# Moving the tiles of a transformer layer onto lines of 128 bytes, with one set of operands 64 bytes off

## The chip, the cores and the metric

The kernel runs on one core of one Trainium2 chip. The metric is the time of one execution on the device in microseconds (us), from three runs. One further execution was recorded by the hardware profiler; every row of a trace in this document is from such a profiled execution. A place in the on-chip memory (SBUF) is given as the byte address inside one of its 128 partitions; "32 mod 128" means that the address leaves 32 when divided by 128.

## The reference, cut to what matters

One layer of an encoder over 512 tokens of width 2048, all in fp32:

```python
mod = silu(c) @ w_ada + b_ada                    # six vectors of 2048: sh1, sc1, g1, sh2, sc2, g2
h = rms_norm(x, norm1_g) * (1.0 + sc1) + sh1
proj = h @ w_in                                  # 2048 x 7168
o_hg = hgrn2_mixer(...)                          # 8 heads of 128, gated linear recurrence
o_sb = stick_breaking_mixer(...)                 # 8 heads of 128, causal attention
x = x + g1 * (concatenate([o_hg, o_sb], -1) @ w_out)
h = rms_norm(x, norm2_g) * (1.0 + sc2) + sh2
gate, up = split(h @ w_ffn_in, 2)                # 2048 x 11264: the first feed-forward product
x = x + g2 * ((silu(gate) * up) @ w_ffn_out)     # 5632 x 2048: the second
```

## The kernel before, in words

**Products in two halves.** Each large product is made of fp32r matmuls. Both operands are split into a high part (rounded to fp32r) and a low part (the rest), and each piece of the product is three matmuls: high by high, high by low, low by high (`three`, `product`, `multiply`). The weights come in by DMA as fp32 into one of four raw tiles (`raw_tile`, L171); `split` (L212 to L222) makes the high part on ScalarE (L220) and the low part on VectorE (L221). The split weights go into a ring of three tiles `hi` and three tiles `lo` in the pool `wp`. In the first feed-forward product every fourth split goes instead into the pair `hi2`, `lo2` of the pool `tp`, which lies at the other end of SBUF (`spare_here`, L1105). The trace calls these operands ff_3hi and ff_3lo, where those of the ring are ff_3h and ff_3l. In the second product every fourth split goes into an unused part of the tile `opsB` (`spare_there`, L1165).

**Stages, in order.** (1) `st`: the hg values for all heads, 16 steps of 24 matmuls with 512 columns, while the first vector of the modulation is computed. (2) `sbp`: eight projections for the attention heads, 1,536 matmuls with 384 columns, with the attention itself between them. (3) `hgf`, `hgq`, `hgg`: projections for the recurrent heads, 1,152 matmuls with 512 columns, with the recurrence between them. (4) `wo`: the output projection, 720 matmuls with 512 columns and, for its last tile, 96 with 256. (5) `ff`, `ffA`, `ffB`, `ffC`: the first feed-forward product, for the tile pairs f = 0 and 1 as 384 plain matmuls, for f = 2 to 43 with Strassen's seven products in place of eight (the operands 1 to 7 of the table `H`), each of 24 matmuls with 256 columns: 42 x 7 x 24 = 7,056. (6) `foA`, `foB`, `foC`: the second feed-forward product in the same way, 1,848 matmuls with 512 columns, and the output.

In stages 3 to 5 a matmul's stationary operand (the one loaded into the array) is a split weight, and its moving operand (the one streamed past it) is an activation: `hhi`/`hlo`, `ohi`/`olo`, `opA` to `opD`. In stages 1, 2 and 6 it is the other way round, and the weight moves. `opA` to `opD` are the seven Strassen operands; `opsA` to `opsC` are those of the second product. Several of these share a place: `hhi`, `ohi`, `opB`, `opsC` in tag `hhi`; `hlo`, `olo`, `opC`, `opsB` in `hlo`; `opA`, `opsA` in `b1`; `opD`, `yraw` in `b22`.

**Places.** Pools are laid down from the left end of SBUF in the order in which they are opened, those with `side="right"` from the right end, and each tile is rounded up to 32 bytes. In the compiled program of this kernel the operands lie thus:

| tiles | first address | mod 128 |
|---|---|---|
| raw tiles | 11,040 | 32 |
| `hi`, `lo` (six tiles of 4,096 bytes) | 43,808 | 32 |
| `hhi`, `ohi`, `opB`, `opsC` | 68,384 | 32 |
| `hlo`, `olo`, `opC`, `opsB` | 101,152 | 32 |
| `opA`, `opsA` | 133,920 | 32 |
| `opD` | 166,688 | 32 |
| `hi2`, `lo2` | 215,008 and 219,104 | 96 |
| `ffS` (sums of weight halves) | 195,552 | 96 |
| `xo`, `x1`, `O` (right end) | 196,576 | 96 |

Inside these tiles every operand of a matmul starts a multiple of 512 bytes from the tile's start, so that its place mod 128 is that of its tile.

The order of the instructions on each engine is fixed when the program is built. On TensorE's queue the small matmuls of attention and recurrence are put between those of the projections by a planner (`Clock`, `Timed`, the times in `Y`) which knows nothing of places.

Of the kernel before, what the change touches and what calls it, by code (L numbers as in the profile page):

```python
# [10 lines left out]
F32 = mybir.dt.float32  # L11
F32R = mybir.dt.float32r
# [5 lines left out]
P = 128  # L18
D = 2048
KT = 16  # L20
T = 512
# [3 lines left out]
HT = 256  # L25
HALF = 8
CHUNKS = (3, 3, 4, 4, 4, 4)
ORDER = (2, 1, 7, 6, 4, 5, 3)
AHEAD = 300
SC2_EARLY = 8  # L30
HG_TASKS = 8
EARLY = 3
# [3 lines left out]
EPS = 1e-6  # L36
# [93 lines left out]
def trunk(ctx, tc, a):  # L130
    nc = tc.nc
    V, S, G = nc.vector, nc.scalar, nc.gpsimd
# [2 lines left out]

    const = ctx.enter_context(tc.tile_pool(name="const", bufs=1))
    wp = ctx.enter_context(tc.tile_pool(name="wp", bufs=3))
    xctx = ctx.enter_context(ExitStack())
    xop = xctx.enter_context(tc.tile_pool(name="xop", bufs=1, side="right"))
    hp = ctx.enter_context(tc.tile_pool(name="hp", bufs=1))  # L140
    dram = ctx.enter_context(tc.tile_pool(name="dram", bufs=1, space=bass.MemoryType.DRAM))
    psum = ctx.enter_context(tc.tile_pool(name="psum", bufs=4, space=bass.MemoryType.PSUM))

    def acc(name):
        return psum.tile([P, T], F32, tag="acc", name=name)
# [9 lines left out]
    ones = const.tile([P, P], F32, name="ones")  # L155
    G.memset(ones, 1.0)
    one = ones[:, 0:1]
    epsb = const.tile([P, 1], F32, name="epsb")
    G.memset(epsb, EPS)
    lead = const.tile([P, 2], F32, name="lead")  # L160
    left = [KT] * 6
    mod = const.tile([P, 96], F32, name="mod")
    gain1 = const.tile([P, KT], F32, name="gain1")
# [48 lines left out]
    def split(r, shape, name):  # L212
# [3 lines left out]
        else:  # L216
            hi = wp.tile(shape, F32R, tag="hi", name=name + "h")
            lo = wp.tile(shape, F32R, tag="lo", name=name + "l")
        with tc.high_priority(offset=AHEAD):
            S.copy(hi, r)  # L220
# [32 lines left out]
        newton(y, av, tmp)  # L253


    hhi = hp.tile([P, KT, T], F32R, tag="hhi", name="hhi")
    hlo = hp.tile([P, KT, T], F32R, tag="hlo", name="hlo")
    xo = xop.tile([P, KT, T], F32, tag="xo", name="xo")
    vctx = ctx.enter_context(ExitStack())
    vp = vctx.enter_context(tc.tile_pool(name="vp", bufs=1))  # L260
# [531 lines left out]
        gates[h] = SG  # L792


    ohi = hp.tile([P, KT, T], F32R, tag="hhi", name="ohi")
    olo = hp.tile([P, KT, T], F32R, tag="hlo", name="olo")
    last = NH - 1

    def split_o(k):
# [36 lines left out]
    fh = ctx.enter_context(tc.tile_pool(name="fh", bufs=1, reuse_waits="tile"))  # L836
    fg = ctx.enter_context(tc.tile_pool(name="fg", bufs=1, reuse_waits="tile"))
# [35 lines left out]

    early = fh.tile([P, 2, HALF, 2, HT], F32R, tag="b1", name="opA")
    H = {1: early[:, 0], 2: early[:, 1], 3: fg.tile([P, HALF, 2, HT], F32R, tag="b22", name="opD")}
    parts = {}

    def block(kh, th, j):  # L880
# [42 lines left out]
    for i, hs in enumerate(halves):  # L923
        out = acc(f"wo{m}h{i}")[:, 0:HT]
        n = 0
# [55 lines left out]
            with tc.high_priority(offset=AHEAD):  # L981
                hold(0)

    late = hp.tile([P, 2, HALF, 2, HT], F32R, tag="hhi", name="opB")
    later = hp.tile([P, 2, HALF, 2, HT], F32R, tag="hlo", name="opC")
    H.update({6: late[:, 0], 7: late[:, 1], 5: later[:, 0], 4: later[:, 1]})
    for j in range(HALF):
        V.tensor_sub(block(0, 0, j), block(0, 1, j), block(0, 0, j))
# [33 lines left out]
    places, blocks = [], [{} for _ in units]  # L1022
# [19 lines left out]
    yraw = []  # L1042

    def begin_second():
        places.append(fh.tile([P, 4, 4, 2, HT], F32R, tag="b1", name="opsA"))
        load_op(0, 0)
        load_y(0, 2)
        load_op(0, 1)
        load_y(0, 0)
        yraw.append(hp.tile([P, 3, 4, T], F32, tag="hhi", name="yraw0"))  # L1050
        load_y(0, 1)
        load_y(0, 3)
        load_op(0, 2)
        load_op(0, 3)
        places.append(hp.tile([P, 4, 4, 2, HT], F32R, tag="hlo", name="opsB"))
        for q in range(4, 7):
            load_op(0, q)
        yraw.append(fg.tile([P, 2, 4, T], F32, tag="b22", name="yraw"))

    rest += [partial(ada, G2, k) for k in range(KT)]  # L1060

# [37 lines left out]
    later = []  # L1099
# [9 lines left out]
    count[0] = 0  # L1109
    with tc.high_priority(offset=AHEAD):  # L1110
        hold(1)
# [118 lines left out]
    for u, (c, i) in enumerate(units):  # L1230
# [15 lines left out]
        for q, p in enumerate(ORDER):  # L1246
# [37 lines left out]
            if p == 3:  # L1284
                load_y(u + 1, 3)
            if u == 0 and q == 6:
                places.append(hp.tile([P, 4, 4, 2, HT], F32R, tag="hhi", name="opsC"))
            if q < 4 and i == (c == 0):
                load_op(c + 1, q)
            if i == 1 and 1 <= q < 4:  # L1290
# [61 lines left out]
```

## Time and profile before

| | |
|---|---|
| median of three runs | 2299.24 us (2299.24 to 2306.46) |
| the profiled execution | 2301.37 us |
| its span, first to last instruction | 2299.2 us |
| mean granted TensorE clock | 0.994 |
| busy: TensorE, weight loads, VectorE, ScalarE | 98%, 89%, 83%, 50% of the span |

Matmuls are pipelined: in the trace one with 256 columns lasts some 280 ns, but the next starts long before it ends. What a matmul costs is the distance from its start to the next one's start, and it is read from the first column of the timeline.

### The profile page before, as it was taken

The page shows a single profiled execution, that of the slowest core. Times are in us where ns is not written, and L with a number is a line of the kernel's source. Part 1 is how long each engine was busy: PE and PEld are TensorE (multiplying, and loading weights), DVE is VectorE, ACT ScalarE, POOL GpSimd, SP SyncE. Part 2 cuts the span into 40 slices and gives each one's busy share as a digit, 9 for nine tenths or more (in the row PEclk, how much of TensorE's full clock was granted, in tenths as well). Part 3 has the DMA queues.
Part 4 walks back from the last instruction along what each step waited for, and adds up shares of the span by engine and source line. Part 5 has one row for each costly group of instructions (what it writes and reads, how often), then busy time and mean ns, then how long its engine had stood idle before and what let it go on. Part 6 is the DMA issues. An engine that isn't in the chain of part 4 may idle for free.

```text
span 2299.2 us, 35729 instructions
## 1 busy us (share of the span) xinstructions
PE 2249.4 (98%) x14171; PEld 2050.2 (89%) x14171; DVE 1917.8 (83%) x2566; ACT 1160.6 (50%) x2015; POOL 10.7 (0%) x25
## 2 busy tenths in 40 slices
PE   7999899999999999999999999999999999999999
PEld 6899899888888788999999999999999977778787
DVE  8887779999888865699899988888888778888888
ACT  4316666565655522564454445454545544544453
POOL 0000000000000000000000000000000000000000
PEclk9999999999999999999999999999999999999999
DMA  9885546853322386346555645454443486665452
GB/s 368 319 317 218 174 145 227 304 183 111 128 93 74 130 303 214 105 151 225 189 204 185 220 143 175 143 174 143 150 160 129 166 314 232 238 220 213 154 200 76
DMA packets 114978, 437.69 MB, mean 190 GB/s; under 512 B 9822, under 2 KB 58236, under 8 KB 76796
## 3 DMA queue, kind: packets, MB, share of 16 engines
q1 hardware_dynamic: 114812, 435.42, 53.0%
q8 instruction: 111, 1.82, 0.3%
q14 instruction: 55, 0.45, 0.1%
HBM read 386.61 MB, written 48.77 MB: 189 GB/s over the span
## 4 chain that ended last, share of the span: by engine, by line
PE 77%; DVE 13%; DMA 3%; issue 3%; ACT 3%; SPq 0%; DVEq 0%; ACTq 0%
PE ffA L93 18%; PE foA L93 9%; PE ffC L93 9%; PE sbp L93 7%; PE wo L93 7%; PE foC L93 4%; PE ffB L93 4%; PE st L93 4%; PE hgf L93 4%; PE hgq L93 3%; PE hgg L93 3%; DMA opd<-fhi 1%; DVE ada L180 1%; DVE yraw L1190 1%; PE l L93 1%
## 5 line engine op out<-in xcount | busy, mean ns | idle before, releaser
L180 DVE SCALAR_TENSOR_TENSOR ada<-ada,cond 128x2048 f32<-128x2048 f32 x95 | 216.8, 2286 | 54.5 <-DMA ada<-in_w_ada 54.3
L93 PE MATMUL ffA<-opD,ff_3h 128*128 128x256 f32 x512 | 93.9, 284 | 1.8 <-ACT u L1018 1.7
L93 PE MATMUL ffA<-opB,ff_6h 128*128 128x256 f32 x512 | 94.1, 284 | 1.0 <-ACT ff_6h L220 1.0
L93 PE MATMUL ffB<-opA,ff_2h 128*128 128x256 f32 x512 | 93.5, 283 | 0.0
L93 PE MATMUL ffC<-opC,ff_4h 128*128 128x256 f32 x512 | 93.5, 283 | 0.0
L93 PE MATMUL ffA<-opC,ff_5h 128*128 128x256 f32 x496 | 90.7, 283 | 0.8 <-ACT b L1018 0.8
L93 PE MATMUL ffA<-opA,ff_1h 128*128 128x256 f32 x496 | 90.6, 283 | 0.0
L93 PE MATMUL ffC<-opB,ff_7h 128*128 128x256 f32 x496 | 90.6, 283 | 0.0
L221 DVE TENSOR_TENSOR wfo_0l<-wfo,wfo_0h 128x1024 fp32r<-128x1024 f32 x48 | 58.7, 1224 | 37.9 <-ACT wfo_0h L220 37.5
L93 PEld LDWEIGHTS ffA<-opD,ff_3h 128*128 128x128 f32 x512 | 79.7, 192 | 2.4 <-ACT u L1018 2.4
L93 PEld LDWEIGHTS ffA<-opB,ff_6h 128*128 128x128 f32 x512 | 80.1, 193 | 1.3 <-ACT ff_6h L220 1.2
L93 PEld LDWEIGHTS ffC<-opC,ff_4h 128*128 128x128 f32 x512 | 79.7, 192 | 0.0
L93 PEld LDWEIGHTS ffB<-opA,ff_2h 128*128 128x128 f32 x512 | 79.7, 192 | 0.0
L220 ACT CAST wfo_0h<-wfo 128x1024 fp32r<-128x1024 f32 x48 | 50.6, 1054 | 57.5 <-PE foA L93 50.4
L1092 ACT CAST fhi<-forms 128x512 fp32r<-128x512 f32 (+1 forms) x63 | 43.6, 692 | 68.5 <-DMA opd<-fhi 59.2
L93 PEld LDWEIGHTS ffA<-opC,ff_5h 128*128 128x128 f32 x496 | 77.2, 192 | 1.0 <-ACT b L1018 1.0
L93 PEld LDWEIGHTS ffC<-opB,ff_7h 128*128 128x128 f32 x496 | 77.3, 192 | 0.0
L93 PEld LDWEIGHTS ffA<-opA,ff_1h 128*128 128x128 f32 x496 | 77.2, 192 | 0.0
L93 PE MATMUL ffA<-opB,ff_6l 128*128 128x256 f32 x256 | 72.7, 284 | 0.0
L93 PE MATMUL ffC<-opC,ff_4l 128*128 128x256 f32 x256 | 72.4, 283 | 0.0
L93 PE MATMUL ffA<-opD,ff_3l 128*128 128x256 f32 x256 | 72.4, 283 | 0.0
L93 PE MATMUL ffB<-opA,ff_2l 128*128 128x256 f32 x256 | 72.4, 283 | 0.0
(1646 smaller groups left out, 7764.6 us busy)
## 6 DMA issues: line engine op xcount, KB each, us to landing
ada<-in_w_ada SPq DMA_DIRECT2D x95, 1024.0 KB, 5.2
wfo<-in_w_fo SPq DMA_DIRECT2D x16, 1024.0 KB, 5.9
yraw<-in_w_fo SPq DMA_DIRECT2D x16, 1024.0 KB, 4.8
fix<-in_w_fix SPq DMA_DIRECT2D x14, 1024.0 KB, 5.6
opd<-forms SPq DMA_DIRECT2D x44, 256.0 KB, 4.3
opd<-fhi SPq DMA_DIRECT2D x42, 256.0 KB, 4.3
opsC<-opd SPq DMA_DIRECT2D x10, 1024.0 KB, 5.1
opsA<-opd SPq DMA_DIRECT2D x9, 1024.0 KB, 7.2
```

The costliest lines, as they stand in the source:

```text
L93: self.engine.matmul(out, lhsT, rhs, **kw)
L180: V.scalar_tensor_tensor(w, w, 1.0, row, op0=ALU.mult, op1=ALU.mult, accum_out=col)
L220: S.copy(hi, r)
L221: V.tensor_sub(lo, r, hi.bitcast(F32))
L1092: S.copy(hi, R[:, q])
L1190: V.tensor_sub(*(t[:, k0:k0 + w] for t in (d, e, g)))
```

## The change

A pool `edge` of 96 bytes is opened first at the right end; the constant `epsb` moves into it. `lead` grows from 2 to 34 elements. The tiles for the operands get 32 elements (128 bytes) more than they hold, and a new function returns a view that begins a given number of elements into such a tile: 16 elements (64 bytes) for `opA` to `opD`, none for all others. No instruction is added, removed or moved.

```diff
+ROOM = 32
+OFF_H, OFF_O, OFF_F, OFF_X = 0, 0, 16, 0
...
+    edge = ctx.enter_context(tc.tile_pool(name="edge", bufs=1, side="right"))
...
+    def offset(pool, shape, dtype, tag, name, shift):
+
+        n = int(np.prod(shape[1:]))
+        t = pool.tile([P, n + ROOM], dtype, tag=tag, name=name)[:, shift:shift + n]
+        axes = "abcd"[:len(shape) - 1]
+        sizes = dict(zip(axes, shape[1:]))
+        return t.rearrange(f"p ({' '.join(axes)}) -> p {' '.join(axes)}", **sizes)
...
-    epsb = const.tile([P, 1], F32, name="epsb")
-    G.memset(epsb, EPS)
-    lead = const.tile([P, 2], F32, name="lead")
+    epsw = edge.tile([P, 24], F32, name="epsw")
+    G.memset(epsw, EPS)
+    epsb = epsw[:, 0:1]
+    lead = const.tile([P, 34], F32, name="lead")
...
-    hhi = hp.tile([P, KT, T], F32R, tag="hhi", name="hhi")
-    hlo = hp.tile([P, KT, T], F32R, tag="hlo", name="hlo")
+    hhi = offset(hp, [P, KT, T], F32R, "hhi", "hhi", OFF_H)
+    hlo = offset(hp, [P, KT, T], F32R, "hlo", "hlo", OFF_H)
...
-    ohi = hp.tile([P, KT, T], F32R, tag="hhi", name="ohi")
-    olo = hp.tile([P, KT, T], F32R, tag="hlo", name="olo")
+    ohi = offset(hp, [P, KT, T], F32R, "hhi", "ohi", OFF_O)
+    olo = offset(hp, [P, KT, T], F32R, "hlo", "olo", OFF_O)
...
-    early = fh.tile([P, 2, HALF, 2, HT], F32R, tag="b1", name="opA")
-    H = {1: early[:, 0], 2: early[:, 1], 3: fg.tile([P, HALF, 2, HT], F32R, tag="b22", name="opD")}
+    early = offset(fh, [P, 2, HALF, 2, HT], F32R, "b1", "opA", OFF_F)
+    H = {1: early[:, 0], 2: early[:, 1], 3: offset(fg, [P, HALF, 2, HT], F32R, "b22", "opD", OFF_F)}
...
-    late = hp.tile([P, 2, HALF, 2, HT], F32R, tag="hhi", name="opB")
-    later = hp.tile([P, 2, HALF, 2, HT], F32R, tag="hlo", name="opC")
+    late = offset(hp, [P, 2, HALF, 2, HT], F32R, "hhi", "opB", OFF_F)
+    later = offset(hp, [P, 2, HALF, 2, HT], F32R, "hlo", "opC", OFF_F)
...
-        places.append(fh.tile([P, 4, 4, 2, HT], F32R, tag="b1", name="opsA"))
+        places.append(offset(fh, [P, 4, 4, 2, HT], F32R, "b1", "opsA", OFF_X))
...
```

`opsB`, `opsC` and the two `yraw` tiles are changed in the same way, with an offset of 0.

## Rows read from the trace of the kernel before

**Rows 1.** Page, parts 1 and 2: busy time of each engine, and the granted clock.

```profile
PE 2249.4 (98%) x14171; PEld 2050.2 (89%) x14171; DVE 1917.8 (83%) x2566; ACT 1160.6 (50%) x2015; POOL 10.7 (0%) x25
...
PEclk9999999999999999999999999999999999999999
```

**Rows 2.** Page, part 4: the chain that ended last, shares of the span.

```profile
PE 77%; DVE 13%; DMA 3%; issue 3%; ACT 3%; SPq 0%; DVEq 0%; ACTq 0%
```

**Rows 3.** Busy time by stretch: PE, PEld, DVE, ACT, POOL; then clock, DMA share, GB/s.

```profile
0.00:100.00 100.00, 88.22 (x382) 72.66 (x383) 83.50 (x126) 44.67 (x59) 1.68 (x9) 1.00 0.95 354
...
440.00:770.00 330.00, 327.22 (x1674) 274.89 (x1672) 288.25 (x540) 200.90 (x444) 9.05 (x16) 1.00 0.36 131
770.00:950.00 180.00, 177.28 (x820) 146.16 (x818) 111.03 (x137) 54.59 (x85) 0.00 (x0) 1.00 0.62 218
950.00:1015.00 65.00, 60.57 (x489) 59.13 (x488) 63.43 (x154) 54.00 (x124) 0.00 (x0) 1.00 0.27 94
...
1400.00:1849.00 449.00, 449.00 (x3796) 449.00 (x3796) 364.66 (x412) 224.82 (x326) 0.00 (x0) 1.00 0.46 159
1849.00:2299.00 450.00, 435.61 (x1917) 352.05 (x1916) 379.23 (x433) 211.91 (x269) 0.00 (x0) 0.99 0.56 201
```

**Rows 4.** Timeline of TensorE, first feed-forward product: start us, us, then engine, line, operands, count.

```profile
1303.62 0.40 PE L93 MATMUL ffA<-opC,ff_5h 128*128 128x256 f32 x2
...
1306.50 0.39 PE L93 MATMUL ffC<-opC,ff_4hi 128*128 128x256 f32 x2
...
1309.11 0.28 PE L93 MATMUL ffC<-opC,ff_4lo 128*128 128x256 f32 x1
```

**Rows 5.** Timeline of TensorE, output projection, 512 columns.

```profile
850.18 0.39 PE L93 MATMUL wo<-olo,wo_8h 128*128 128x512 f32 x1
850.40 0.39 PE L93 MATMUL wo<-ohi,wo_8l 128*128 128x512 f32 x1
...
852.90 0.39 PE L93 MATMUL wo<-olo,wo_0h 128*128 128x512 f32 x1
```

**Rows 6.** Timeline of TensorE, attention projection, 384 columns.

```profile
149.97 0.33 PE L93 MATMUL sbp<-wsb_2h,hhi 128*128 128x384 f32 x1
...
151.53 0.33 PE L93 MATMUL sbp<-wsb_2h,hhi 128*128 128x384 f32 x1
```

**Rows 7.** Timeline of TensorE where the clock is at half: two groups, 256 columns.

```profile
1016.21 0.63 PE L93 MATMUL ffC<-opB,ff_7hi 128*128 128x256 f32 x2
1016.64 0.41 PE L93 MATMUL ffC<-opB,ff_7lo 128*128 128x256 f32 x1
...
1018.13 0.63 PE L93 MATMUL ffA<-opB,ff_6h 128*128 128x256 f32 x2
1018.56 0.41 PE L93 MATMUL ffA<-opB,ff_6l 128*128 128x256 f32 x1
```

**Rows 8.** Busy time and clock in that stretch.

```profile
1015.80:1018.70 2.90, 2.90 (x15) 2.90 (x15) 2.90 (x3) 0.42 (x1) 0.00 (x0) 0.50 0.00 0
```

**Rows 9.** Timeline of TensorE: a plain fp32 group of the recurrence, 256 columns.

```profile
511.45 1.03 PE L93 MATMUL r<-QB_w,KB_w 128*128 128x256 f32 x4
```

**Rows 10.** Groups by line: count, busy us, mean ns of one, idle before.

```profile
L93 PE MATMUL r<-QB_w,KB_w 128*128 128x256 f32 x8 | 2.0, 378 | 0.0
L93 PE MATMUL ffA<-opC,ff_5h 128*128 128x256 f32 x496 | 90.7, 283 | 0.8 <-ACT b L1018 0.8
L93 PE MATMUL ffA<-opC,ff_5hi 128*128 128x256 f32 x176 | 30.6, 277 | 0.0
```

**Rows 11.** Timeline of the weight loads, output projection (compare group 5).

```profile
850.18 0.19 PEld L93 LDWEIGHTS wo<-ohi,wo_8l 128*128 128x128 f32 x1
850.41 0.19 PEld L93 LDWEIGHTS wo<-ohi,wo_0h 128*128 128x128 f32 x1
```

**Rows 12.** Groups by line: the two splits, from tiles at 96 and at 32 mod 128.

```profile
L221 DVE TENSOR_TENSOR wfo_0l<-wfo,wfo_0h 128x1024 fp32r<-128x1024 f32 x48 | 58.7, 1224 | 37.9 <-ACT wfo_0h L220 37.5
L220 ACT CAST wfo_0h<-wfo 128x1024 fp32r<-128x1024 f32 x48 | 50.6, 1054 | 57.5 <-PE foA L93 50.4 <-PE ffC L93 2.4 <-DVE wfo_2l L221 2.0
L221 DVE TENSOR_TENSOR ff_5l<-ffS,ff_5h 128x1024 fp32r<-128x1024 f32 x31 | 37.8, 1218 | 0.0
L220 ACT CAST ff_5h<-ffS 128x1024 fp32r<-128x1024 f32 x31 | 32.5, 1050 | 36.6 <-PE ffA L93 36.6
```

**Rows 13.** Busy time by stretch inside the first feed-forward product, columns as in group 3.

```profile
1200.00:1300.00 100.00, 99.94 (x842) 99.72 (x842) 91.93 (x103) 48.49 (x71) 0.00 (x0) 1.00 0.54 195
...
1500.00:1600.00 100.00, 100.00 (x848) 100.00 (x847) 82.42 (x93) 50.73 (x74) 0.00 (x0) 1.00 0.47 161
```

More of the change, by code (lines that the diff above doesn't have):

```diff
@@ L1049, in begin_second @@
         load_y(0, 0)
-        yraw.append(hp.tile([P, 3, 4, T], F32, tag="hhi", name="yraw0"))
+        yraw.append(offset(hp, [P, 3, 4, T], F32, "hhi", "yraw0", 0))
         load_y(0, 1)
@@ L1054, in begin_second @@
         load_op(0, 3)
-        places.append(hp.tile([P, 4, 4, 2, HT], F32R, tag="hlo", name="opsB"))
+        places.append(offset(hp, [P, 4, 4, 2, HT], F32R, "hlo", "opsB", OFF_X))
         for q in range(4, 7):
             load_op(0, q)
-        yraw.append(fg.tile([P, 2, 4, T], F32, tag="b22", name="yraw"))
+        yraw.append(offset(fg, [P, 2, 4, T], F32, "b22", "yraw", 0))
     rest += [partial(ada, G2, k) for k in range(KT)]
@@ L1286, in trunk @@
             if u == 0 and q == 6:
-                places.append(hp.tile([P, 4, 4, 2, HT], F32R, tag="hhi", name="opsC"))
+                places.append(offset(hp, [P, 4, 4, 2, HT], F32R, "hhi", "opsC", OFF_X))
             if q < 4 and i == (c == 0):
```

## The prediction

> **What bounds the kernel now.** I read the shares first: TensorE is busy 98% of the span at a clock that is nearly always full [rows 1], and the chain of work that ended last runs over TensorE for 77%, over VectorE for 13% [rows 2]. The stretches say the same stage by stage: in the second half of the first feed-forward product TensorE is busy 449.00 of 449 us, in the output projection 177 of 180, in the second feed-forward product 436 of 450 [rows 3]. Two stretches differ. In the first 100 us the DMA engines are busy 95% at 354 GB/s, beside a TensorE busy 88%; from 950 to 1015 us VectorE is busy 63.43 of 65 us [rows 3]. So outside those two, what a matmul costs is what the kernel costs.
>
> What a matmul costs is read from starts. In the first feed-forward product a group of 24 with weights from the ring (place 32 mod 128, moving operand at 32 too) goes from 1303.62 to 1306.50 us: 2.88 / 24 = 120.0 ns each. The next group has its weights in `hi2`, `lo2` (96, moving operand still at 32): from 1306.50 to the start of its last at 1309.11 there are 23 distances, 2.61 / 23 = 113.5 ns [rows 4]. 256 columns at 2.4 GHz take 106.7 ns, so the excess is 13.3 ns (32 cycles) in the first group and 6.8 ns (16 cycles) in the second. With 512 columns and both operands at 32, twelve distances take 2.72 us, 226.7 ns each, against 213.3: again 13.3 [rows 5]. With 384 columns nine take 1.56 us, 173.3 against 160: again 13.3 [rows 6]. The excess is thus the same per matmul at every width, and it halves when the two operands lie 64 bytes apart mod 128. The groups show that this is no accident of one product: 283 ns for 496 matmuls, 277 for 176 of the other kind [rows 10]. Where the clock is at half, two matmuls take 0.43 us, 215 ns each, in both kinds, and 213.3 is what 256 columns need at 1.2 GHz [rows 7, 8]. In plain fp32, four records take 1.03 us, the last of them 378 ns by its group, so three distances take 0.65 us, 217 ns, for 256 columns at two cycles each [rows 9, 10]. [...]
>
> **The change part by part.** No instruction is added or removed; addresses move. `epsb` leaves the left end and `lead` grows from 32 to 160 bytes, so all that follows on the left goes up by 96: 11,040 becomes 11,136 = 87 x 128, and raw tiles and the ring lie on lines; each operand tile then takes 128 bytes more, and the later ones stay on lines. At the right end `edge` pushes everything down by 96: from 96 to 0 mod 128, `hi2` and `lo2` too. So the first feed-forward product gets weights at 0 and moving operands at 64, all other fp32r products 0 and 0.
>
> *First feed-forward product, 7,056 matmuls of 256 columns.* Every fourth of the 294 splits goes to `hi2`: 73 x 24 = 1,752 matmuls at 113.5, the other 5,304 at 120.0, sum 835.3 us, which with few waits is the stage that ends at 1849 us. The new pair (0, 64) is nowhere in the trace. Its distance is the cheap one, so at most 113.5; the 16 cycles that then remain have one candidate left, the start in the middle of a 64-byte piece (32 and 96 both are), and it goes too. The lower bound is 106.7 plus the 2 to 3 ns that the slow streams keep; I take 109.3. That is 771.2 us, 64.1 less; the bounds are 35 (113.5 for all) and 82 (106.7). VectorE eats some of it: up to f = 17 it also does a modulation row for each f and is busy 91.93 of 100 us [rows 13]. An f takes 168 matmuls, 19.84 us now, with 18.2 us of VectorE; at 109.3 it takes 18.36, and VectorE would be at 99%. It can't be that dense with its waits on ScalarE's high parts, so I give back 0.25 us for each of 16 f: 60 us are left. From f = 18 it is busy 82.42 of 100, which becomes 89% and hides.
>
> *The 384 plain matmuls before it* stand in the stretch where VectorE is busy 63.43 of 65 us [rows 3]: of up to 4 us I take 1. *The last output tile*, 96 matmuls of 256 columns: 1 us.
>
> *All others, 0 and 0.* The start is mended, the distance is not. [...] If that still costs, 6.7 ns are saved per matmul; if it cost only because the moving stream had a piece too many, all but 2.6 ns go: 10.7. Both come from the rows above and nothing is nearer; I take the middle, 8.7 ns (for 384 columns too).
> - Attention projections: 1,536 x 8.7 = 13.4 us; attention stands between them, I keep 80%: 10.7.
> - `st`: 384 x 8.7 = 3.3, but DMA is busy 95%: 1 [rows 3].
> - Recurrent projections: 1,152 x 8.7 = 10.0; VectorE is busy 288 of 330 us: 7 [rows 3].
> - Output projection: 720 x 8.7 = 6.3; VectorE has room (111 of 180): 6 [rows 3].
> - Second feed-forward product: 1,848 x 8.7 = 16.1; VectorE is busy 379 of 450: 14 [rows 3].
>
> *VectorE, ScalarE, DMA.* Their operands move too. The splits cost 1224 and 1054 ns from tiles at 32, 1218 and 1050 from a tile at 96 [rows 12]: within half a percent, so nothing. The transfers keep their sizes; nothing. `epsb` and `lead` are touched a few times: nothing, and were a few tenths of a us lost, the DMA wait at the start would hide it.
>
> Sum: 60 + 1 + 1 + 10.7 + 1 + 7 + 6 + 14 = 101 us. The profiled execution took 2301.4 us (span 2299.2), 2 above the median of the runs, so the median goes to 2299.2 - 101 = **2198 us**.
>
> [...] With weights at 96 in place of 32 and nothing else changed, a matmul is 6.5 ns shorter [rows 4]; so the weight's place reaches the moving stream. [...]
>
> **The rivals.**
> - *Only the distance counts, not the line.* All of the first feed-forward product comes to 113.5 (5,304 x 6.5 = 34 us), the 0-and-0 products stay as they are: 2264 us with a us for the plain 384. For it: distance is all that the rows vary. Against it: an excess of 16 cycles would be left in a pair that lies well.
> - *Two streams on one line collide for the whole 32 cycles.* Only the 64-byte offset gains: 61 us, 2238.
> - *64 bytes is half a line of 128.* The first feed-forward product stops at 113.5 and the rest gains: 34 + 40 = 74 us, 2225.
> - *The pair at the other end of SBUF is cheap because of its region, and no place mod 128 matters.* Then nothing changes: 2299. For it: `hi2` is the only tile at 96 that feeds a matmul here, and it lies some 170,000 bytes from the ring. Against it: exactly 16 cycles.
> - *Slower: the weight's own place sets the price.* 96 costs 16 cycles and 32 costs 32, so by a straight line 0 costs 40 (16.7 ns): ring products lose 3.3 ns, `hi2` products 9.9, the 5,640 others 3.3: 17.5 + 17.3 + 18.6 = 53 us, 2352. It decides once weights at 0 cost over 28 cycles, today's mean of the first feed-forward product; nothing shows 0.
>
> **How the numbers follow.** Forecast 0.52, distance alone 0.15, collision 0.12, half line 0.07, nothing 0.08, slower 0.06. The forecast by itself spans 2172 (10.7 for the others, nothing lost to VectorE) to 2210 (6.7 and more lost). Going up, the range takes in 2225, 2238 and 2264; leaving out 2299 and 2352 (0.14) and a little at the low end gives 2172 to 2266. Some 0.3% is what a measurement here tells from no change. Faster: 0.52 + 0.15 + 0.12 + 0.07 = 0.86; same 0.08; slower 0.06.
>
> **What would show it.** In the profile after, groups of 24 in the first feed-forward product should take 2.62 us, ring and `hi2` alike; 2.72 means distance alone or half a line, 2.88 nothing. Output projection matmuls should start 216 to 220 ns apart; 226.7 means the collision. VectorE should be busy over 97% between 1000 and 1300 us, with waits of TensorE on the low parts. The prediction is wrong if TensorE's distances shrink and its waits on VectorE take the gain back, or if they don't shrink.

## The result, and the profile after

The changed kernel took 2311.3 us (median of six runs, 2307.61 to 2312.69) beside 2303.38 us for the kernel before (six runs, 2299.24 to 2306.46; the first three of them are those shown above): ratio 1.0035, 95% interval 1.0023 to 1.0046. It is slower by a third of a per cent, where a time 4.4% under the median shown was forecast. The profiled execution took 2311.36 us, span 2309.2 us.

The page, part 1, and the shares of the chain that ended last:

```profile
PE 2253.2 (98%) x14171; PEld 2037.6 (88%) x14171; DVE 1915.4 (83%) x2566; ACT 1156.1 (50%) x2015; POOL 10.8 (0%) x25
...
PE 69%; DVE 17%; DMA 7%; issue 4%; ACT 3%; SPq 0%; DVEq 0%; ACTq 0%
```

Counts and shares are those of before, to the instruction [rows 1]; each engine also has the same instructions in the same order. But TensorE's part of the chain fell from 77 to 69%, and DMA's rose from 3 to 7% [rows 2]: something new waits on transfers. Busy time by stretch (PE, PEld, DVE, ACT, POOL, then clock, DMA share, GB/s):

```profile
770.00:950.00 180.00, 176.30 (x775) 140.94 (x774) 110.57 (x135) 55.45 (x87) 0.00 (x0) 1.00 0.60 212
...
1400.00:1849.00 449.00, 445.27 (x3806) 442.67 (x3806) 368.62 (x419) 223.31 (x329) 0.00 (x0) 1.00 0.45 154
```

In the second half of the first feed-forward product TensorE has 3,806 matmuls where it had 3,796, and is idle 3.7 us where it was never idle [rows 3]. In the output projection's window it is nearly as busy (176.3 us for 177.3) and has fewer, 775 for 820; part of that is the stage's start, 3 us later.

The matmuls themselves, from the timeline of TensorE (start us, duration us, engine, line, operands, count). First feed-forward product, a group with `opB`, then one with `opC`:

```profile
1308.87 0.40 PE L95 MATMUL ffC<-opB,ff_7h 128*128 128x256 f32 x2
...
1311.70 0.40 PE L95 MATMUL ffA<-opC,ff_5h 128*128 128x256 f32 x2
...
1314.43 0.39 PE L95 MATMUL ffC<-opC,ff_4hi 128*128 128x256 f32 x2
```

From 1308.87 to 1311.70 there are 24 distances with `opB`: 2.83 us, 117.9 ns each. From 1311.70 to 1314.43 there are 24 with `opC`: 2.73 us, 113.8 each. The ring and `hi2` no longer differ; which moving operand a group has now decides. 2.62 us for 24, as forecast, is nowhere. VectorE, forecast to be busy over 97% from 1000 to 1300 us, was busy 276.2 of the 300. Output projection, 512 columns:

```profile
854.94 0.40 PE L95 MATMUL wo<-olo,wo_0h 128*128 128x512 f32 x1
855.18 0.39 PE L95 MATMUL wo<-ohi,wo_0l 128*128 128x512 f32 x1
855.41 0.40 PE L95 MATMUL wo<-ohi,wo_0h 128*128 128x512 f32 x1
...
857.74 0.40 PE L95 MATMUL wo<-olo,wo_0h 128*128 128x512 f32 x1
```

Twelve distances take 2.80 us, 233.3 ns, against 226.7 before [rows 5] and 216 to 220 forecast: a loss.

Stage by stage, from the start of a stage's first matmul to that of its last, in us:

| stage | before | after | lines_only | off_lines | room_256 |
|---|---|---|---|---|---|
| `st`, 512 columns | 88.7 | 91.5 | 89.7 | 91.2 | 89.0 |
| `sbp`, 384 columns | 338.3 | 335.6 | 335.8 | 335.4 | 335.7 |
| recurrent projections, 512 | 327.9 | 330.2 | 328.2 | 330.2 | 327.2 |
| output projection, 512 | 173.2 | 177.1 | 173.1 | 178.7 | 173.2 |
| first feed-forward product, 256 | 893.4 | 893.4 | 902.5 | 890.5 | 892.3 |
| second feed-forward product, 512 | 445.5 | 448.9 | 445.3 | 447.7 | 445.3 |

After against before: +2.8 - 2.7 + 2.3 + 3.9 + 0 + 3.4 = 9.7 us, of the 10.0 between the two profiled executions. Each column is one execution, and a stage can differ by some 3 us from one to the next without any change in its matmuls: the output projection took 176.1 us in `before_two_fhi` (below), whose matmuls there cost 227.0 ns as before. The prices are steadier. The mean distance between starts of neighbouring matmuls of a stage, those over 245 ns left out, went from 226.7 to 231.7 ns in `st`, from 228.2 to 231.8 in the recurrent projections, from 227.0 to 233.0 in `wo` and from 227.5 to 229.7 in the second feed-forward product. So two things are to be explained: why products of 512 columns lose, and why 256 columns gain nothing although their matmuls got shorter.

### The profile page after: what moved, and what is told of

Read it like the earlier page. It is cut to its first block, busy times and chain, and to the rows that moved or that the text cites. A ratio compares the mean times of both kernels' runs of the same rounds, so it can differ in the third digit from the quotient of the medians.

```text
span 2309.2 us, 35729 instructions
## 1 busy us (share of the span) xinstructions
PE 2253.2 (98%) x14171; PEld 2037.6 (88%) x14171; DVE 1915.4 (83%) x2566; ACT 1156.1 (50%) x2015; POOL 10.8 (0%) x25
## 4 chain that ended last, share of the span: by engine, by line
PE 69%; DVE 17%; DMA 7%; issue 4%; ACT 3%; SPq 0%; DVEq 0%; ACTq 0%
PE ffA L95 11%; PE sbp L95 9%; PE foA L95 9%; PE wo L95 7%; PE ffC L95 6%; PE foC L95 4%; PE st L95 4%; PE hgf L95 4%; PE hgq L95 3%; PE hgg L95 3%; DMA opd<-fhi 3%; PE ffB L95 3%; DVE yraw L1202 1%; PE l L95 1%; DVE ff_5l L233 1%
## 5 line engine op out<-in xcount | busy, mean ns | idle before, releaser
L1104 ACT CAST fhi<-forms 128x512 fp32r<-128x512 f32 (+1 forms) x63 | 43.7, 693 | 123.9 <-DMA opd<-fhi 88.4
L1105 DVE TENSOR_TENSOR forms<-forms,fhi 128x512 fp32r<-128x512 f32 (+1 forms) x63 | 48.9, 776 | 37.7 <-ACT fhi L1104 37.5
```

The source lines that it names most:

```text
L1104: S.copy(hi, R[:, q])
L1105: V.tensor_sub(R[:, q].bitcast(F32R), R[:, q], hi.bitcast(F32))
```

## The experiments

In what follows the distance is the place of the moving operand less that of the stationary one, mod 256 bytes. "Lateness" is worked out from the 7,056 starts of the Strassen part of the first feed-forward product: all distances between starts over 124 ns, each less the mean of the rest, summed; the mean of the rest is the "mean matmul". Lateness is more than waiting. Of the changed kernel's 26.9 us, 19.3 stand at starts before which TensorE sat idle for over 0.12 us. Another 2.1 stand at the start next after such a wait, which comes some 222 ns after it, and 3.1 in two stretches at a granted clock of 0.50, from 1021.7 and from 1113.8 us, both soon after waits of 2.6 to 2.8 us; the kernel before has one such stretch there, from 1015.5 us.

**Does the line of 128 bytes do anything?** In `lines_only` every operand lies on a line and none is 64 bytes off:

```diff
-ROOM = 32
-OFF_H, OFF_O, OFF_F, OFF_X = 0, 0, 16, 0
+ROOM = 64
+OFF_H, OFF_O, OFF_F, OFF_X = 0, 0, 0, 0
```

> The changed kernel with 256 spare bytes per operand tile in place of 128 and no offset anywhere: all tiles on lines, every pair of operands at distance 0 mod 256. If the line counts, as the prediction had it: 512 columns at 216 to 220 ns, 384 at 163 to 167, some 30 to 50 us faster than before. If only the distance counts: 512 columns at 226.7 and 384 at 173 to 174 as before, the first feed-forward product at 120.0 in all products; the quarter that was cheap loses 6.6 ns x 1,752 = 11.6 us, so the kernel comes out some 10 us slower than before (about 2311).

2310.27 us, ratio 1.0043 (1.0026 to 1.0059). Timelines of TensorE, first feed-forward product and output projection:

```profile
1309.57 0.40 PE L95 MATMUL ffA<-opD,ff_3h 128*128 128x256 f32 x2
...
1312.45 0.40 PE L95 MATMUL ffA<-opA,ff_1h 128*128 128x256 f32 x2
...
850.04 0.39 PE L95 MATMUL wo<-ohi,wo_0l 128*128 128x512 f32 x1
...
852.76 0.39 PE L95 MATMUL wo<-ohi,wo_0l 128*128 128x512 f32 x1
```

2.88 us for 24 (120.0 ns) and 2.72 for 12 (226.7): to the digit the prices at 32 mod 128 [rows 4, 5]. The groups with `hi2` cost 120.0 here too, and that quarter's loss of 6.5 ns, 11.4 us, less 2.4 us of lateness, is the 9 us of the stage. A start on the line is worth nothing.

The other way round, `off_lines` keeps the offsets of the change and takes the lines away:

```diff
-    edge = ctx.enter_context(tc.tile_pool(name="edge", bufs=1, side="right"))
...
-    epsw = edge.tile([P, 24], F32, name="epsw")
...
-    lead = const.tile([P, 34], F32, name="lead")
+    epsb = const.tile([P, 1], F32, name="epsb")
...
+    lead = const.tile([P, 2], F32, name="lead")
```

> The changed kernel with its first part undone: epsb and lead as before and no pool edge, so that the ring and the operands lie off lines again (32 mod 128), with the same distances between them as in the changed kernel; only the pair hi2, lo2 comes to other distances (128 and 0 in place of 64 and 192), which costs 1 to 7 ns for each of its 1,752 matmuls. If the line counts, it differs from the changed kernel in every stage. If only the distance counts, the 512-column stages are as long as in the changed kernel (output projection 177 us, first stage 91) and the whole takes 2310 to 2320.

2309.95 us, ratio 1.0034 (1.0024 to 1.0044): as the change, with the same loss in `st` and `wo` (table). Line or no line, the products of 512 columns lose. This also shifts `hi2` against the rest, and its groups then cost 118.8 ns (distance 128) and 119.6 to 119.9 (distance 0).

**What does the place do?** `place_scan` holds nothing of the layer, only one weight tile, one activation tile and groups of matmuls at all pairs of starts:

```python
for n, count in ((256, 24), (512, 12), (384, 16)):
    for w in range(0, 256, 32):
        for m in range(0, 512, 32):
            group(f"n{n}w{w}m{m}_", w, m, n, count)   # weight at w, moving operand at m
```

> This kernel computes none of the layer: it splits x into two tiles and issues groups of fp32r matmuls, 24 of 256 columns, 12 of 512 or 16 of 384 to a group, nothing else running. Each group has one place w of the stationary operand and one place m of the moving one, w in steps of 32 bytes over 256, m in steps of 32 over 512 (and in steps of 8 at w = 0); the last groups alternate two places of the moving operand as the output projection does. Read: the distance of starts in each group. If the line counts, as the prediction had it (a start inside a 64-byte piece costs 16 cycles, equal halves of a 128-byte line another 16): 109 to 110 ns for 256 columns wherever w and m are multiples of 64 and differ by 64 mod 128, 113 where they are equal mod 128, and 120 only where m lies off a multiple of 64. If only the distance m - w mod 256 counts: equal rows along each diagonal, 120 at distance 0 on lines and off them, 113 to 114 at one distance of 64 and 117 to 118 at the other, over 120 at 128; then 512 columns show 227 at distance 0 and 229 to 238 at 128. If places don't count and the region of the tile does (the fourth rival): one number for all groups of a width, since all lie in the same two tiles.

Its timeline; each row is a group, and the weight is at 0 while the moving operand starts at 0, 32, 64 and so on (256 columns, then 512):

```profile
33.07 3.04 PE L33 MATMUL n256w0m__169<-X,W 128*128 128x256 f32 x24
35.95 3.00 PE L33 MATMUL n256w0m__194<-X,W 128*128 128x256 f32 x24
...
47.33 2.98 PE L33 MATMUL n256w0m__294<-X,W 128*128 128x256 f32 x24
50.15 2.89 PE L33 MATMUL n256w0m__319<-X,W 128*128 128x256 f32 x24
52.88 3.00 PE L33 MATMUL n256w0m__344<-X,W 128*128 128x256 f32 x24
55.71 3.04 PE L33 MATMUL n256w0m__369<-X,W 128*128 128x256 f32 x24
...
395.61 2.89 PE L33 MATMUL n512w0m__3369<-X,W 128*128 128x512 f32 x12
398.34 2.97 PE L33 MATMUL n512w0m__3382<-X,W 128*128 128x512 f32 x12
...
406.71 2.96 PE L33 MATMUL n512w0m__3421<-X,W 128*128 128x512 f32 x12
409.51 2.96 PE L33 MATMUL n512w0m__3434<-X,W 128*128 128x512 f32 x12
```

From one start to the next: 2.88 us at distance 0, 2.83, 2.83, 2.87 up to 96, 2.85 at 128, 2.82, 2.73 at 192, 2.83, and 55.71 begins the same series again. Inside the groups, per matmul: 120.0, 117.6, 117.8, 120.1, 118.9, 117.5, 113.4, 118.3 ns for distances 0 to 224. With 512 columns it is 226.7 at 0 and 228.5 to 235 everywhere else, 233.4 at 128; with 384, 173.3 to 176.7, and 173.3 at several distances. The grid's other rows give the same numbers along its diagonals to within some 2 ns with 256 and 512 columns (with 384, 3.5 ns), but for distance 192 with 256 columns, which costs 113.3 in most rows and 117.8 in some: the difference counts and not the places, its period is 256 bytes, and the best distance is not the same for 256 and 512 columns. The prediction's 106.7 to 109.3 occurs nowhere, not in steps of 8 bytes either, which the same run holds for 256 columns.

`place_regions` repeats the groups with the weights in five tiles, the first at 44,032 and the last at 219,648 in SBUF:

```python
for name, W in (("A", WA), ("B", WB), ("C", WC), ("D", WD), ("E", WE)):
    for s in (0, 32, 224):
        for d in range(0, 256, 32):
            group(f"w{name}s{s}d{d}_", W, X, s, (s + d) % 256 + 256 * (s == 224), 256, 24)
```

> This kernel computes none of the layer: groups of 24 fp32r matmuls of 256 columns in the pattern of the first feed-forward product (high by high, high by low, low by high), the weights taken from five tiles that begin at 44,032, 150,016, 186,368, 204,288 and 219,648, distances m - w from 0 to 224 by 32, starts of w at 0, 32 and 224 mod 256; some groups with the moving operand in the last tile, and some of 512 columns. If the distance mod 256 alone sets the cost, every tile gives the same eight numbers as the scan before (120.0, 117.6, 117.8, 120.1, 118.9, 117.5, 113.4, 118.3 at 0, 32, ... 224). If the region of the tile counts too, the tiles beyond some address give these numbers shifted to other distances: 113.4 at distance 64 from 219,648 would explain the cheap quarter of the kernel before, whose weights lay at 224 mod 256 and its moving operands at 32, a distance of 64.

Its timeline for distance 192 and the group behind it, in the first tile and in the last:

```profile
56.04 2.89 PE L47 MATMUL wAs0d__341<-X,WA 128*128 128x256 f32 x24
58.77 3.00 PE L47 MATMUL wAs0d__366<-X,WA 128*128 128x256 f32 x24
...
327.40 2.89 PE L47 MATMUL wEs0d__2741<-X,WE 128*128 128x256 f32 x24
330.13 3.00 PE L47 MATMUL wEs0d__2766<-X,WE 128*128 128x256 f32 x24
```

2.73 us in both. The same prices come in every tile and at every start, but for distance 32, which costs 116.5 or 117.8 in every tile, and they come too with the moving operand in the last tile: the region, the prediction's fourth rival, falls. But distance 64, which costs 113.5 in `hi2` of the kernel before, costs 117.8 here.

`place_states` asks whether one distance can have two prices. It puts short odd matmuls (40 to 232 columns) ahead of the groups, to enter each of them differently:

```python
for n, count, step in ((256, 24, 16), (512, 12, 32)):
    for d in range(0, 256, step):
        for i, kick in enumerate((0, 40, 72, 104, 136, 168, 200, 232)):
            if kick:
                group(f"k{n}d{d}i{i}_", 0, d, kick, 2)
            group(f"s{n}d{d}i{i}_", 0, d, n, count)
...
```

> This kernel computes none of the layer: the scan again, with each distance entered in several ways. In the run with distance 192, matmuls of the first feed-forward product took 113.4 ns in some stretches and 117.7 in others at the same places, and the number changed only where TensorE had waited. Here each group of 24 (or 12 of 512 columns) follows two short matmuls of 40 to 232 columns, or a group at another distance. If a distance has one cost, each distance gives one number however it is entered. If the two streams can lock into more than one rhythm, distances 64 and 192 give both 113.4 and 117 to 118, distance 0 gives 120.0 always; then the cheap quarter of the kernel before (distance 64, entered from distance 0) is the good rhythm of that distance, and the groups 'distance 0, then 64' give 113.4.

Its timeline where distance 64 is entered after 200 and after 232 columns (names `s`; a group ends where the next row starts):

```profile
150.05 3.01 PE L33 MATMUL s256d64i__1221<-X,W 128*128 128x256 f32 x24
152.90 0.38 PE L33 MATMUL k256d64i__1246<-X,W 128*128 128x232 f32 x2
153.12 2.89 PE L33 MATMUL s256d64i__1249<-X,W 128*128 128x256 f32 x24
155.85 3.03 PE L33 MATMUL s256d80i__1274<-X,W 128*128 128x256 f32 x24
```

2.85 and 2.73 us. With 256 columns distance 0 costs 120.0 after each of the eight entries; distance 64 costs 117.8 after seven and 113.3 after one; distance 192 costs 113.3 after six and 117.8 after two; distance 112 settles at 113.3 after all eight, though only 3 to 13 matmuls after the start of the group. So some distances have two rhythms, and what happened before picks one. Entering distance 64 from distance 0, as the kernel before does, gave 117.8, where 113.4 was expected: a miss. These groups take their weights in plain order, though, not high, high, low as the kernel does, and none of the runs with groups alone enters the kernel's order at 64 from distance 0.

The kernel before itself has both rhythms at distance 64: of its 73 groups with `hi2`, 69 cost 113.5 ns and four 117.7. In `before_two_fhi` (below) it is 71 and two. Of these six slow groups four follow upon a start over 124 ns; of the 140 fast ones none does.

`place_fine` goes down to 16 bytes (512 and 384 columns) and 4 bytes (256 columns, 96 to 128), with four entries each:

```python
for n, count, ds in ((512, 12, range(0, 256, 16)), (384, 16, range(0, 256, 16)), (256, 24, range(96, 129, 4))):
    for d in ds:
        for i, kick in enumerate((0, 40, 104, 168)):
            ...
```

> This kernel computes none of the layer: the scan of places once more, 512 and 384 columns at distances in steps of 16 bytes, each entered in four ways, and 256 columns from 96 to 128 in steps of 4. If the cheapest distance is the same for all widths, 512 columns show 220 ns (213.3 and 16 cycles) at 112 and 384 columns 167. If the width matters, 0 stays the cheapest for 512 columns with 226.7, and nothing is to be had there.

Its timeline at distances 108, 112, 116 (names `s`; a group ends where the next row starts):

```profile
449.77 2.99 PE L33 MATMUL s256d108i__2704<-X,W 128*128 128x256 f32 x24
452.60 0.29 PE L33 MATMUL k256d108i__2729<-X,W 128*128 128x40 f32 x2
...
461.74 2.93 PE L33 MATMUL s256d112i__2813<-X,W 128*128 128x256 f32 x24
464.51 0.29 PE L33 MATMUL k256d112i__2838<-X,W 128*128 128x40 f32 x2
...
473.43 3.11 PE L33 MATMUL s256d116i__2922<-X,W 128*128 128x256 f32 x24
476.37 0.30 PE L33 MATMUL k256d116i__2947<-X,W 128*128 128x40 f32 x2
```

2.83, 2.77 and 2.94 us; inside the groups 117.8, 113.3 and 123 ns. Four bytes beside the best place lies one of the worst. With 512 columns 0 stays the best (226.7 once settled; 231.2 at 112; 226.7 to 236.7 at 240, by the entry), and with 384 columns 0 and 112 both settle at 173.3.

**Why do the products of 512 columns lose?** `ROOM` is 128 bytes, so each operand tile shifts the next by 128 mod 256. With the first addresses of before, the 96 bytes and the spare bytes, the ring and the tile of `hhi`, `ohi` lie at 128 mod 256, that of `hlo`, `olo` at 0: of three matmuls two are at distance 0 and one at 128. (In the second feed-forward product the pairs at 128 are `opsB` with the ring, and `opsA` or `opsC` with weights in `opsB`: they cost 232 to 233 ns, the other pairs 227 to 229.) `room_256` doubles the spare bytes and changes nothing else:

```diff
-ROOM = 32
+ROOM = 64
```

> The changed kernel with 256 spare bytes per operand tile in place of 128, nothing else: on lines and 64 bytes off as before, but neighbouring operand tiles no longer 128 bytes apart mod 256. If the distance mod 256 sets the cost, all products but the first feed-forward one are back at distance 0: 226.7 for 512 columns, and the 10 us that these stages lost come back; the first feed-forward product stands at distance 64 with 113.4 to 117.8. Together 2295 to 2302, 10 to 15 us faster than the changed kernel. If the changed kernel lost its time to something else than these 128 bytes, it stays near 2310.

2298.23 us, ratio 0.9983 (0.9973 to 0.9993). All five stages of 512 and 384 columns are within 2.6 us of before (table), their matmuls cost what they cost before (227.0 in `wo`, for 233.0), and the 10 us are back. That was the loss.

**Where did the gain of the shorter matmuls of 256 columns go?** In the changed kernel the 128 spare bytes put `opA`, `opB` at distance 64 and `opC`, `opD` at 192. Their mean is 116.2 ns, 2.2 less than before, 16 us over 7,056 matmuls; and lateness went from 10.5 to 26.9 us. Waits of TensorE in the changed kernel from 1015 to 1856 us (in all, times, longest), then the first for before, 1015 to 1849 us:

```profile
PE ffC L95 <- ACT c L1030: 6.3, 9, 2.8
PE ffA L95 <- ACT u L1030: 3.2, 4, 1.1
PE ffC L95 <- ACT ff_7hi L232: 2.6, 1, 2.6
PE ffA L95 <- ACT b L1030: 1.4, 4, 0.8
```

```profile
PE ffA L93 <- ACT u L1018: 1.7, 2, 1.5
```

TensorE waits for ScalarE's copies `a`, `b`, `c`, `u`, which take `ffA` to `ffC` out of the tiles that it has to fill again, and, in this stretch, not for VectorE's low parts. Timeline of ScalarE in the changed kernel, and of TensorE beside it:

```profile
1157.90 0.62 ACT L1104 CAST fhi<-forms 128x512 fp32r<-128x512 f32 x1 [4.36 <-DMA opd<-fhi]
1158.42 0.37 ACT L1030 COPY u<-ffA 128x256 f32<-128x256 f32 x1
...
1157.46 0.28 PE L95 MATMUL ffC<-opC,ff_4lo 128*128 128x256 f32 x1
1158.84 0.51 PE L95 MATMUL ffA<-opD,ff_3h 128*128 128x256 f32 x2 [1.11 <-ACT u L1030]
```

ScalarE stands 4.36 us at the cast into `fhi`, since the store of the previous one out of the only buffer has not landed; the copy `u` is behind it in the queue, and TensorE behind `u`. The groups by line, in the changed kernel and then in the kernel before:

```profile
L1104 ACT CAST fhi<-forms 128x512 fp32r<-128x512 f32 (+1 forms) x63 | 43.7, 693 | 123.9 <-DMA opd<-fhi 88.4 <-DVE forms L1096 30.1 <-DVE forms L1105 3.1
...
L1092 ACT CAST fhi<-forms 128x512 fp32r<-128x512 f32 (+1 forms) x63 | 43.6, 692 | 68.5 <-DMA opd<-fhi 59.2 <-DVE forms L1093 4.3 <-DVE forms L1084 4.0
```

88.4 us of standing on that store, where the kernel before has 59.2. In the versions with one buffer it grows on the whole as the matmuls get faster: 37.6 us in `lines_only` (120.0 ns), 59.2 before (118.4), 58.2 in `off_lines` and 75.3 in `room_256` (117.6 and 117.7), 88.4 in the changed kernel and 76.4 in `dist_192` (116.2 and 115.7), 91.7 in `dist_112` (113.6). To see whether this is the limiter, first the distance was made better. `dist_192` takes 192 for all operands of the product, `dist_192_two_fhi` adds a second buffer:

```diff
-ROOM = 32
-OFF_H, OFF_O, OFF_F, OFF_X = 0, 0, 16, 0
+ROOM = 64
+OFF_H, OFF_O, OFF_F, OFF_X = 0, 0, 48, 0
...
-                hi = tp.tile([P, b - a, HT], F32R, tag="fhi", name=f"fhi{f}_{a}", bufs=1)
+                hi = tp.tile([P, b - a, HT], F32R, tag="fhi", name=f"fhi{f}_{a}", bufs=2)
```

> The same with an offset of 192 bytes for the operands of the first feed-forward product: distance 192 there, 0 everywhere else. If only the distance counts: 113.4 ns there in all products against a mean of 118.4 before, 7,056 x 5.0 = 35 us less matmul time, all other stages as before. If TensorE's waits in that stage don't grow: about 2266. If they eat what a faster stream gains, as in the changed kernel (17 us less matmul time, the stage as long as before): 2285 to 2299. If the line counts: 30 to 50 us faster than before from the other stages, with 216 to 220 ns for 512 columns.

> The same with two buffers for the tile fhi, so that the cast into it need not wait until the store of the one before has landed. If TensorE's waits in the first feed-forward product come from ScalarE's queue standing at that cast (the copies that free the accumulators are queued behind it), they shrink, and this one is 5 to 15 us faster than the one with one buffer. If they come from VectorE being full (18.2 us of each 19.1 in the first 16 steps), the two take the same time.

2294.74 us, ratio 0.9979 (0.9966 to 0.9992), and 2293.79, ratio 0.9965 (0.9945 to 0.9984): the second buffer shows no difference that the intervals can tell, where 5 to 15 us were expected: a miss. The timeline of TensorE in `dist_192` shows why one distance is no safe price:

```profile
1537.07 0.40 PE L95 MATMUL ffA<-opC,ff_5h 128*128 128x256 f32 x2
...
1539.19 0.40 PE L95 MATMUL ffA<-opC,ff_5h 128*128 128x256 f32 x2
...
1540.05 0.50 PE L95 MATMUL ffC<-opC,ff_4hi 128*128 128x256 f32 x2 [0.34 <-ACT c L1030]
...
1540.86 0.39 PE L95 MATMUL ffC<-opC,ff_4hi 128*128 128x256 f32 x2
...
1542.90 0.39 PE L95 MATMUL ffA<-opD,ff_3h 128*128 128x256 f32 x2
```

From 1537.07 to 1539.19 there are 18 matmuls, 117.8 ns each; after a wait of 0.34 us, from 1540.86 to 1542.90, again 18, 113.3 each. The distance is 192 throughout. The rhythm changed across the wait. That is no single case: in `dist_192` the price goes from one rhythm to the other 13 times and in `dist_192_two_fhi` five times, and each of these changes lies at a start over 124 ns. It fits that the runs of `dist_192_two_fhi` reach from 2277.39 to 2298.32 us.

Distance 112 was the fast one without a second rhythm (113.3 ns after all eight entries), and so it was tried in the kernel (`OFF_F` 28, that is 112 bytes; `ROOM` 64), without and with the second buffer:

> The changed kernel with 256 spare bytes per operand tile and an offset of 112 bytes for the operands of the first feed-forward product: distance 112 there, 0 elsewhere. In the runs that measure places alone, distance 112 took 113.3 ns however it was entered, distance 192 took 113.3 or 117.8. If that holds in the layer: 113 to 114 ns in all seven products, 35 us less matmul time than before (distance 192 had 115.7, 19 us less). How much of it stays shows what else bounds the stage: with distance 192 it ended 6 us shorter than before; if waits take the same share, this one gains 10 to 12 us (about 2290); if the stage is bound by ScalarE's queue or VectorE already, it gains no more than distance 192 did (2294).

> The same with two buffers for the tile fhi. If TensorE's waits in this stage come from ScalarE standing at the cast into fhi until the store before it has landed, the copies that free the accumulators come sooner, and this one is 8 to 15 us faster than the one with one buffer (about 2278). If VectorE is what is full, the two take the same time.

2295.13 us, ratio 0.9982 (0.9973 to 0.9991), and **2277.53 us, ratio 0.9899 (0.9886 to 0.9912)**, which beats both kernels by more than any other version here. What ScalarE waited for at the cast into `fhi` from 1015 to 1856 us (in all, times, longest), without and with the second buffer:

```profile
ACT fhi L1104 <- DMA opd<-fhi: 91.7, 38, 4.4
ACT fhi L1104 <- DVE forms L1096: 35.1, 20, 3.1
```

```profile
ACT fhi L1104 <- DMA opd<-fhi: 24.6, 20, 4.5
ACT fhi L1104 <- DVE forms L1096: 12.5, 14, 2.5
```

TensorE's lateness at starts that waited for ScalarE fell from 26.7 to 15.0 us with it.

Is it then the buffer alone that won? `before_two_fhi` is the kernel before with that one edit:

> The kernel before with a second buffer for fhi and no place moved, so that its operands keep distance 0 (120.0 ns for three quarters of the first feed-forward product) and 64 (113.4 ns for the rest). Theory (what dist_112_two_fhi won is mostly the cheaper matmul, and the buffer only keeps the queue of ScalarE from taking it back): in the kernel before the starts of that product are only some 10 us later in sum than its own rhythm would have them, so the buffer alone can give at most that: 2294 to 2300 us, ratio 0.997 to 1.000, with matmuls at a mean of 118 ns still. Rival (the buffer is what won, whatever the distance): 2280 us or less, ratio about 0.990, as dist_112_two_fhi.

2299.92 us, ratio 0.999 (0.9981 to 1.0): no. And does the buffer give the changed kernel its gain back? `after_two_fhi` and `room_256_two_fhi` make the same edit in the change and in `room_256`:

> The changed kernel with a second buffer for fhi and nothing else. Theory (the queue behind the cast into fhi takes back most of the 16 us that the cheaper matmuls give, and the stages of 512 columns lose 10 us, which stay lost): the waits of the first feed-forward product go from 27 us to some 15, so 2298 to 2304 us, ratio 0.997 to 1.001, with wo at 177 us still. Rival (what the matmuls gain is lost elsewhere, to VectorE or to starts that merely alternate between two distances): 2309 to 2313 us, ratio 1.003 to 1.005.

> room_256 (256 spare bytes in place of 128, the 64-byte offset kept, so that products of 512 columns are at distance 0 again) with a second buffer for fhi. Theory: room_256 without it was at 2298 us with 15 us of waits; the buffer takes some 5 of them, 2290 to 2296 us, ratio 0.995 to 0.998. Rival (the buffer does nothing at this distance): as room_256, ratio 0.998.

2301.02 us, ratio 1.0001 (0.9988 to 1.0015), and 2295.41, ratio 0.9978 (0.9969 to 0.9986). The first lies clear of the change's own 1.0023 to 1.0046, so the queue did cost it some 0.3%; in the second the intervals overlap. The Strassen part of the first feed-forward product in the profiled executions:

| kernel | distances | mean matmul, ns | lateness, us | length, us |
|---|---|---|---|---|
| before | 0 and 64 | 118.4 | 10.5 | 845.6 |
| before_two_fhi | 0 and 64 | 118.4 | 12.0 | 847.1 |
| lines_only | 0 | 120.0 | 8.1 | 854.7 |
| after | 64 and 192 | 116.2 | 26.9 | 846.5 |
| after_two_fhi | 64 and 192 | 117.7 | 15.5 | 845.7 |
| room_256 | 64 | 117.7 | 14.7 | 844.9 |
| room_256_two_fhi | 64 | 117.8 | 10.4 | 841.3 |
| dist_192 | 192 | 115.7 | 24.6 | 840.6 |
| dist_192_two_fhi | 192 | 116.1 | 15.4 | 834.3 |
| dist_112 | 112 | 113.6 | 38.3 | 839.4 |
| dist_112_two_fhi | 112 | 113.5 | 21.8 | 822.3 |

Two columns have to be read together: among the kernels with one buffer the lateness on the whole grows as the matmuls get faster, and the second buffer takes 4 to 17 us of it away except in the kernel before. In the profiled execution of `after_two_fhi` lateness fell by 11 us, but distance 192 ran in its slow rhythm (117.5 in place of 114.0), so this one profile shows no shorter stage. It was also among the slowest of its runs (2308.54 us; they reach from 2293.05 to 2309.16). That the runs with less time had the other rhythm is likely and not shown.

## Why the prediction was wrong

*The step that failed* is "the start is mended, the distance is not", with what it was built on: that of 32 cycles of excess at (32, 32), 16 belong to a start in the middle of a 64-byte piece and 16 to the distance mod 128. There is no part for the start: `lines_only` puts all operands on lines and pays 120.0 and 226.7 ns as before. What varies with the place is the distance alone, and its period is 256 bytes, not 128; at the best distance 113.3 ns are paid, 6.6 over the prediction's 106.7, and no run says what they are. (The rows bear out the 106.7 as what 256 columns more add, 226.7 less 120.0 ns at a granted clock of 1.00; with 384 columns 173.3 ns lie half-way [rows 4 to 6]. That is 0.417 ns a column, which the prediction calls a cycle at 2.4 GHz.) `hi2` at 96 and the ring at 32 looked like places 64 bytes apart mod 128; they were 64 apart mod 256 in a certain order, moving operand ahead of the weight. Two rows cannot carry a rule with two terms: 16 and 32 cycles fit any split. (The 2 to 3 ns that a slow stream was said to keep are rounding at half clock: there the starts are 213 or 214 ns apart, mean 213.3; in plain fp32 they are 215 to 218.)

*First feed-forward product, 60 us.* The new pair did not come to 109.3, but to 117.7 (distance 64) and 114.0 (192). Even 113.5, the prediction's upper bound, is about what the best place gives. So the gain at the matmuls was 16 us and not 64, and lateness, which grew by 16 us, took all of it. The 4 us given back to VectorE named the wrong engine: VectorE is not the queue in which TensorE's copies stand. ScalarE is, which the page gives as 50% busy; 88.4 us of its idle time are spent at the head of its queue, on a store. That standing was in the trace of before (59.2 us) and cost TensorE little there (of 10.5 us of lateness 6.6 stand at waits for ScalarE, in the changed kernel 17.5). With matmuls at 113.6 lateness takes 28 of the 34 us that `dist_112` gains at them.

*All others, 0 and 0: 40 us by 8.7 ns a matmul.* No run shows a saving of 8.7 ns: with 0 and 0 throughout `lines_only` pays 226.7 ns as before. For 512 columns 0 was already the best distance, and the change kept it for some two matmuls in three. The others went to 128, because "each operand tile then takes 128 bytes more, and the later ones stay on lines" was checked mod 128 only. In the output projection a triple costs 0.70 us for 0.68, more than the scan's prices add up to (226.7 twice and 233.4, 0.687 us); in `after_two_fhi` the same stage cost 229.5 ns a matmul, so here too one order has more than one price. The stages of 512 columns lost 12.4 us, and `sbp` came out 2.7 better. That is not its price, which rose from 173.6 to 175.5 ns: its starts over 190 ns, each less that mean, came to 10.4 us in place of 14.6, and in the versions at distance 0 there, with matmuls of 173.6 to 173.7, they scatter from 12.4 to 15.0 us and the stage from 335.6 to 338.4. So the line is no part of it. That the kernel as a whole moved by only 0.3% is chance: 16 us gained at matmuls of 256 columns, 16 lost in lateness and some 10 in the rest.

*The rivals.* "Only the distance counts" was right in its principle and wrong in its period, so its 2264 us was not near. The collision on one line had 226.7 ns at 0 and 0 right (`lines_only`) and wanted 2.62 us for 24 in the first feed-forward product; half a line wanted a gain at 0 and 0. Neither came. The region, by which no place mod 128 matters, forecast no change and so came nearer in time than the forecast. It still isn't what the runs show: `place_regions` pays 2.73 us for 24 at distance 192 in the first tile and in the last, and `place_fine` varies nothing but the distance and pays 113.3 to 123 ns. "The weight's own place sets the price" had the right sign and the wrong cause: weights at 0 cost 120.0, as at 32.

*What stays open.* Why 69 of the 73 groups with `hi2` in the kernel before ran at 113.5 ns: they were entered from distance 0 without a wait, but the same entry gave the slow rhythm in `place_states`. Why the price follows the difference of the two places, and what has a period of 256 bytes, no run shows; nor does any show what a weight load, which starts within 10 ns of the running matmul's start [rows 5, 11], has to do with it. And 21.8 us of lateness are left in `dist_112_two_fhi`, 15.0 of them at waits for ScalarE, which no experiment took away.

## What to carry to other kernels

Before a place is moved for the sake of a price read at two places, scan the price over all places in a kernel of nothing but such matmuls: here it is one run (`place_scan`), and it would have shown both the period of 256 and that no place in steps of 8 bytes costs 109 ns. When spare bytes are added to a tile, work out the new place of every tile behind it, modulo the real period. And when the bound engine is made faster, look not at who is busy, but at which in-order queue ahead of it stands on something: here one more buffer was worth some 1 us at 118 ns a matmul (`before`, `room_256`) and 18 us at 113.5 (`dist_112`).

## What the runs showed of the hardware that was not expected

- The distance between starts of fp32r matmuls of 128 by 256 depends on the difference of the operands' addresses mod 256 bytes: 120.0 ns at 0, 113.3 at 112, 123 at 116 (`place_scan`, `place_fine`). With 512 columns 0 is the best (226.7), and the others cost 228.5 to 235 in the scan.
- Some distances have two rhythms (113.3 or 117.8 ns at 64 and at 192 in `place_states`). At one distance throughout (`dist_192`, `dist_192_two_fhi`) all 18 changes of rhythm lie at a start over 124 ns, one of them at a wait of 0.34 us.
- No price depended on the region of SBUF, with weights from 44,032 to 219,648 (`place_regions`: 2.73 us for 24 at distance 192 in the first tile and in the last), nor on a start on a line of 128 bytes (120.0 and 226.7 ns in `lines_only` as in the kernel before).
